# A two-layer decoder trunk on one core: the first projection by pairs of k-tiles, the heads in five steps, the input's second load later, six plain k-tiles at the borders

## The chip, the cores and the metric

The kernel runs on one core of a Trainium2 chip. The metric is the device time of one execution in microseconds (us), the median of several runs. The profile shown is that of one execution. Five engines work side by side, each through its own queue in order: TensorE (PE, matmuls, and PEld, its weight loads), VectorE (DVE), ScalarE (ACT), GpSimd (POOL) and SyncE (SP), which here issues every DMA.

## The reference, cut to what matters

Two layers, 256 tokens, width 2048, everything in float32. Layer 0 normalises the input, scales and shifts it by vectors made from a conditioning vector `c` (adaLN), multiplies it by one wide matrix and feeds two groups of four heads; layer 1 is a sparse attention. Each layer ends with an MLP.

```python
# adaLN vectors: silu(c) @ ada_w[l] + ada_b[l], six chunks of 2048 columns (shift, scale, gate, twice)
h = rms_norm(x, norm1_g) * (1 + scale) + shift
p = h @ w_in                                  # 256 x 2048 times 2048 x 8200
q_m, k_m (after conv+silu), v_m, o_m, if_m, q_r, k_r, v_r, g_r = split(p)
h_m = mlstm_chunkwise(q_m, k_m, v_m, gates(if_m))      # heads 0 to 3, width 256
h_r = retention_chunkwise(rotary(q_r), rotary(k_r), v_r)   # heads 4 to 7
y = rms_norm_per_head(concat(h_m, h_r)) * gate(o_m, g_r)
x = x + gate_vec * (y @ w_out)
x = x + gate_vec2 * (relu(mod(x) @ w1) ** 2 @ w2)     # then layer 1 likewise
```

## The kernel before

Weights come as k-tiles of 128 rows (16 of them, k = 0 to 15, for a width of 2048). A product in full precision is made in one of two ways. **Plain**: the float32 tile as it landed is multiplied at once (`mm`, line 124); the trace shows each such matmul as two instructions. **Split**: `wsplit` (lines 235 and 237) rounds the tile to `wh` on ScalarE and puts the rest into `wl` on VectorE, the activations `hs` are split likewise, and three fast matmuls (`wh` with both halves of `hs`, `wl` with the high one) give the result. Raw weights pass through four buffers `raw`, four `wh` and four `wl`; the plain tiles of the first stages use all three kinds in a fixed turn (`wraw`).

Stage by stage, with the names that the text uses:

- **Start.** x is loaded (`xn`), its row lengths are taken, it is scaled and transposed into `xT` (line 737). The adaLN shift and scale of the first norm come from 33.6 MB of `ada_w`, by pairs of k-tiles: for pair 0 to 7, `cond_sum` loads 4.2 MB in eight DMAs (`ar`, four buffers) and folds it on VectorE, 16 multiply-adds of 128x512 (lines 752 and 754); `cond_pair` then sums over partitions (four transposes on TensorE, four reductions on ScalarE, lines 335 and 338) and makes the two normalised k-tiles `hf` and their split `hs`.
- **Phase a**: plain products of k-tiles 0 to 3 with the columns of the values 0 to 2 and of one query (1792 columns), summed in PSUM over the four. **Phase b**: plain products of k-tiles 0 to 7 with the output gates and the last values (1536 columns). **Phase c**: all 16 k-tiles with the seven remaining q and k units (1792 columns), k-tiles 0 to 5 plain and 6 to 15 split. `gates()` (the small projection of the mLSTM gates, its scans and weights E) runs at k = 8. Pairs 2 to 7 are folded and normalised in between.
- **Rest of a**: k-tiles 4 to 15, split (12 steps). **Heads**: `segment` makes the remaining columns; when a head has q, k and gate, `mix_head` gives three steps (`scores`, `values`, `gated`), which are put into the list `pending`, and `side()` runs one of them after each piece of matmul work. `values` ends with a Newton square root on VectorE and the scaling `yn` on ScalarE (line 1005), `gated` with transposes of `yn` (line 1013). x is loaded again and transposed (lines 1151 to 1155) between two segments.
- **w_out**, the output projection, adds into `xT`. Meanwhile `Fill` spreads the folds of three more adaLN chunks (96 pieces of 512 KB, line 407) over its calls, one call per step of weights from k = 12 of phase c on.
- **Borders.** `entry` starts the three following projections (two MLPs and layer 1's input) before the norm's length is known: k-tiles 0 to 7 are multiplied plain and unnormalised (`wu`), the other eight split.

Of the kernel before, what the change touches and what calls it, by code (L numbers as in the profile page):

```python
# [23 lines left out]
EPS = 1e-6  # L24
NEG = -3.0e38
# [69 lines left out]
def tile_trunk(ctx: ExitStack, tc: tile.TileContext, io, out):  # L95
# [267 lines left out]
    def ada_rows(acc, hf):  # L363
# [17 lines left out]
        for c in (2 * hf, 2 * hf + 1):  # L381
            pending.extend(turn(c))
# [64 lines left out]
    class Norm:  # L447
# [53 lines left out]
    def entry(W, cols, tiles, norm, l, n, held, late, out, done):  # L501
# [5 lines left out]
        for k0 in range(0, 8, 2):  # L507
# [4 lines left out]
        for k0 in range(0, KT, 2):  # L512
            if k0 >= 8:
                wh, wl = wload(W, k0, 2, cols, PAIRED)
            for q, (c, m) in enumerate(tiles):
                for kk in range(2):
                    k = k0 + kk
                    if k < 8:
                        mm(held[q][0:m, 0:T + 1], ws[k0 // 2][:, kk * w + c:kk * w + c + m], us[k][:, 0:T + 1],
                           k == 0, k == 7)  # L520
                    else:
                        nmul2(q % 2)(late[q // 2], hs[k], wh, wl, kk * w + c, m, k == 8 and q % 2 == 0, k == KT - 1)
            side()
            if k0 == 6:
                for k in range(8, KT):
# [11 lines left out]
        for k in range(8):  # L537
            hs[k] = norm.normed(l, n, k)
        return hs

    def residual(W, nk, hget, gate, norm, groups, stag, fill):

        k0 = 0
        for plan, banks in groups:
# [77 lines left out]
    def mlp(l, before, fill, norm):  # L622
        with ExitStack() as es:
# [13 lines left out]
            def squared(i, a):  # L637
# [7 lines left out]
                       lambda q: squared(q, z[q]))  # L645
            for g in range(1, DFF // 512):
                def evac(j, b, g=g):
# [5 lines left out]
                       [[(j * P, P)] for j in range(4)], evac, banks1, fill=fill, first=8 if g == 1 else 0)  # L653
            if l == 1:
# [3 lines left out]
                zp.tile([P, 24], F32, name="pad")  # L658
# [32 lines left out]
    with ExitStack() as es:  # L691
# [24 lines left out]
        early = [load_ar(0, 0), load_ar(0, 1)]  # L716
# [6 lines left out]
        ss, v, r = st(4, "nv"), st(2, "nw"), st(2, "nr")  # L723
        for t in range(2):
# [31 lines left out]
        def cond_pair(pr):  # L756

            if pr not in sums_of:
                cond_sum(pr)
            acc = sums_of.pop(pr)  # L760
            cs = st(4, "adac")
            row_sums(cs, [acc[:, i // 2, (i % 2) * P:(i % 2 + 1) * P] for i in range(4)])
# [6 lines left out]
            out = {}  # L769
            for k in (2 * pr, 2 * pr + 1):  # L770
# [15 lines left out]

        for s in range(3):
# [3 lines left out]
        nb = sums(6)  # L791
        nb = [nb[2 * i:2 * i + 2] for i in range(3)]
        q0b = bank(2)
        hfs = {}
        for pr in range(PART // 2):
            ws = {}
            hfs.update(cond_pair(pr))
            for k in (2 * pr, 2 * pr + 1):
                ws[k] = [wraw() for _ in range(2)]
                for i, o, (a, b) in zip((0, 1, 1), (0, 0, 512), wcols):  # L800
                    SP.dma_start(ws[k][i][:, o:o + b - a], wE[k * P:(k + 1) * P, a:b])
            for k in (2 * pr, 2 * pr + 1):
# [11 lines left out]
        S.copy(q0, q0b)


        gbs = [lbank() for _ in range(4)]
        vbs = [bank(0), bank(1)]
        wc = {}

        def load_c(k):
            wc[k] = wplain(k, 3072, 4096), wplain(k, 6664, 7176)

        for k in range(PART):
            load_c(k)
            if k % 2 == 1:
                cond_sum((PART + k - 1) // 2)
        for k in range(HALF):
            if k not in wc:
                load_c(k)  # L830
            wa, wb = wc.pop(k)
            a, z = k == 0, k == HALF - 1
            for j in range(8):
                mm(gbs[j // 2][:, j % 2 * T:j % 2 * T + T], wa[:, j * P:(j + 1) * P], hfs[k], a and j % 2 == 0, z)
            for t in range(2):
                mm(vbs[t], hfs[k][:, t * P:(t + 1) * P], wb[:, 0:512], a, z)
            if k % 2 == 1 and k < PART:
                hfs.update(cond_pair((PART + k - 1) // 2))
            elif k % 2 == 1:
                cond_sum((PART + k - 1) // 2)  # L840
        gpart = []
        for j in range(4):
            gpart.append(xT[:, 2 * j:2 * j + 2, :])
            S.copy(gpart[j].rearrange("p e t -> p (e t)"), gbs[j])
        v3 = wp.tile([P, 2, 512], F32, tag="acc", bufs=2, name="v3")
# [550 lines left out]
```

## Time and profile before

| | before |
|---|---|
| median of 3 runs (lowest to highest) | 2325.82 us (2317.92 to 2327.18) |
| the profiled execution's own time | 2326.86 us |
| span from first to last instruction | 2325.1 us |
| TensorE busy share of the span | 97% |
| VectorE, ScalarE | 73%, 51% |
| data read | 607.38 MB |

The span lies inside the execution's own time; 1.8 us are around it. A busy share is an average over stages of different kinds, so stages are read by themselves. Matmuls are pipelined: the mean time of one is longer than the distance from one to the next.

### The profile page before, as it was taken

The numbers are of one execution on the slowest core, as the hardware profiler recorded it, in microseconds if no ns is written. First come the engines' busy times: TensorE is split into PE (matmuls) and PEld (weight loads), VectorE is DVE, ScalarE is ACT, GpSimd is POOL, SyncE is SP. The second block draws the span as 40 slices with busy tenths as digits, with TensorE's granted clock in tenths as the row PEclk, the third lists the DMA queues.
The fourth block names the chain that finished last, engine by engine and source line by source line (L and its number), as shares of the span: only waits on it lengthen the run. The fifth ranks groups of instructions, "written<-read, shape, count | busy, mean of one in ns | idle before, by whom it ended". The sixth has DMA issues, their size and how long they took to land.

```text
span 2325.1 us, 37502 instructions
## 1 busy us (share of the span) xinstructions
PE 2255.0 (97%) x14121; PEld 2008.9 (86%) x14121; DVE 1706.4 (73%) x2499; ACT 1190.4 (51%) x2248; POOL 0.5 (0%) x8
## 2 busy tenths in 40 slices
PE   5899998999999999999999999999999999999999
PEld 3688888999988888899989899999988888888887
DVE  5767897995878777888887789866877455555555
ACT  3225454455565565655555445665655555444443
POOL 0000000000000000000000000000000000000000
PEclk9999999999999999999999999999999999999999
DMA  9998998996699999999899787746878666555554
GB/s 330 353 305 284 304 319 270 329 328 218 215 318 314 317 312 317 307 310 315 279 328 318 251 268 228 247 137 188 272 263 292 182 194 195 190 190 199 191 190 162
DMA packets 268909, 611.97 MB, mean 263 GB/s; under 512 B 26692, under 2 KB 95286, under 8 KB 268728
## 3 DMA queue, kind: packets, MB, share of 16 engines
q1 hardware_dynamic: 268728, 609.59, 78.6%
q8 instruction: 110, 1.80, 0.3%
q14 instruction: 71, 0.58, 0.1%
HBM read 607.38 MB, written 2.12 MB: 262 GB/s over the span
## 4 chain that ended last, share of the span: by engine, by line
PE 81%; DVE 8%; DMA 7%; issue 2%; ACT 2%; SPq 0%; DVEq 0%; ACTq 0%
PE L L124 48%; PE M L124 31%; DMA ada<-in_ada_w_dram 3%; DVE wl L237 2%; DMA raw<-in_even_w_in_dram 2%; DVE acc L407 2%; DVE acc L754 1%; DMA raw<-in_mlp_w_dram 1%; PE M L335 1%; ACT wh L235 1%; DMA xn<-in_x_dram 0%; DVE cv L1065 0%; ACT junk L338 0%; PE M L737 0%; SPq L246 0%
## 5 line engine op out<-in xcount | busy, mean ns | idle before, releaser
L237 DVE TENSOR_TENSOR wl<-raw,wh 128x1024 fp32r<-128x1024 f32 (+1 forms) x724 | 877.6, 1214 | 485.1 <-ACT wh L235 474.9
L235 ACT CAST wh<-raw 128x1024 fp32r<-128x1024 f32 (+1 forms) x724 | 754.0, 1042 | 822.9 <-PE M L124 442.5
L124 PE MATMUL L<-hs,wh 128*128 128x256 f32 (+1 forms) x4608 | 1107.8, 321 | 6.7 <-ACT wh L235 4.4
L124 PE MATMUL L<-hs,wl 128*128 128x256 f32 x3120 | 866.3, 278 | 4.2 <-DVE wl L237 4.2
L124 PEld LDWEIGHTS L<-hs,wh 128*128 128x128 f32 x4608 | 762.2, 189 | 69.5 <-ACT wh L235 5.0
L124 PEld LDWEIGHTS L<-hs,wl 128*128 128x128 f32 x3120 | 587.9, 189 | 7.0 <-DVE wl L237 6.0
L124 PE MATMUL M<-hs,wh 128*128 128x512 f32 (+2 forms) x1816 | 514.8, 345 | 0.0
L124 PE MATMUL M<-hs,wl 128*128 128x256 f32 (+2 forms) x1444 | 401.4, 278 | 0.0
L407 DVE SCALAR_TENSOR_TENSOR acc<-ada,cond,acc 128x1024 f32<-128x1024 f32 x300 | 383.5, 1278 | 18.0 <-DMA ada<-in_ada_w_dram 17.7
L124 PEld LDWEIGHTS M<-hs,wh 128*128 128x128 f32 (+1 forms) x1816 | 313.0, 186 | 50.8 <-issue 1.6
L124 PEld LDWEIGHTS M<-hs,wl 128*128 128x128 f32 (+2 forms) x1444 | 268.9, 186 | 1.9 <-issue 1.1
L124 PE MATMUL L<-wh,zh 128*128 128x512 f32 x512 | 168.6, 389 | 0.0
L124 PE MATMUL M<-wh,zh 128*128 128x512 f32 x512 | 168.5, 389 | 0.0
L124 PEld LDWEIGHTS L<-wh,zh 128*128 128x128 f32 x512 | 96.1, 188 | 20.3 <-issue 0.4
L124 PEld LDWEIGHTS M<-wh,zh 128*128 128x128 f32 x512 | 96.1, 188 | 20.0
L124 PE MATMUL L<-wl,zh 128*128 128x512 f32 x256 | 99.7, 390 | 0.0
L124 PE MATMUL M<-wl,zh 128*128 128x512 f32 x256 | 99.6, 389 | 0.0
L338 ACT ACTIVATE junk<-M 128x128 f32<-128x128 f32 x210 | 55.1, 278 | 84.8 <-PE M L335 84.8
L754 DVE SCALAR_TENSOR_TENSOR acc<-ar,cond,acc 128x512 f32<-128x512 f32 x120 | 90.2, 751 | 5.0 <-DMA ar<-in_ada_w_dram 1.4
L638 ACT ACTIVATE half<-half 128x256 f32<-128x256 f32 x120 | 47.9, 411 | 24.2 <-DVE half L328 24.2
L124 PE MATMUL L<-hf,raw 128*128 128x256 f32 x224 | 53.3, 392 | 4.4 <-DMA raw<-in_even_w_in_dram 4.4
L124 PEld LDWEIGHTS L<-wl,zh 128*128 128x128 f32 x256 | 48.1, 188 | 10.2 <-DVE wl L237 0.3
(273 smaller groups left out, 1578.2 us busy)
## 6 DMA issues: line engine op xcount, KB each, us to landing
raw<-in_mlp_w_dram SPq DMA_DIRECT2D x504, 512.0 KB, 4.5
ada<-in_ada_w_dram SPq DMA_DIRECT2D x320, 512.0 KB, 5.3
raw<-in_even_w_in_dram SPq DMA_DIRECT2D x136, 256.0 KB, 5.2
ar<-in_ada_w_dram SPq DMA_DIRECT2D x64, 512.0 KB, 7.8
raw<-in_odd_w_in_dram SPq DMA_DIRECT2D x48, 512.0 KB, 4.5
raw<-in_even_w_out_dram SPq DMA_DIRECT2D x32, 512.0 KB, 5.2
raw<-in_odd_w_out_dram SPq DMA_DIRECT2D x32, 512.0 KB, 4.2
raw<-in_even_w_in_dram SPq DMA_DIRECT2D x28, 512.0 KB, 5.9
```

The lines of the kernel that those rows point to most:

```text
L124: PE.matmul(o, a, b, start=start, stop=stop, skip_group_check=True)
L235: S.copy(wh[:, :n], raw[:, :n])
L237: last_split[0] = V.tensor_tensor(wl[:, :n], raw[:, :n], wh[:, :n].bitcast(F32), op=OP.subtract)
L335: PE.transpose(b[:, i * P:(i + 1) * P], t, ident)
L338: S.activation(j, b[:, i * P:(i + 1) * P], func, accum_out=dst[:, i:i + 1])
L407: V.scalar_tensor_tensor(acc, r, cond[:, kr:kr + 1], acc, op0=OP.mult, op1=OP.add)
L638: S.activation(a, a, AF.Relu)
L754: V.scalar_tensor_tensor(acc, ar[:, kr], cc, acc, op0=OP.mult, op1=OP.add)
```

## The change

- **Start.** All eight `ar` DMAs of pair 0 are issued at once. Pair 0 is folded on TensorE: 16 plain matmuls whose stationary side is a column of `cond` repeated 32 times (`cond32`), the four of a group writing to four different 32-partition strips of one PSUM bank. The chain of a pair is cut in three: `folds` (loads and folds), `summed` (four matmuls with a column of ones in place of transposes and reductions), `normed`. They are called at separate places.
- **Phases a and b by pairs.** a for k-tiles 0, 1; b for 0, 1; a for 2, 3; b for 2 to 7. The sums of the first pair are copied out, those of the second added by VectorE (13 more additions of 128x512). Loads are called earlier (`load_a`, `load_b`).
- **Phase c.** k-tiles 0 to 3 plain, 4 to 15 split; loads called ahead by `load_q`; `folds` of pair 5, 6, 7 at k = 3, 6, 9, `summed` at k = 2, 5, 8, 11. `gates()` runs at k = 13 and ends after its scans; `score_weights` is called after phase c. `fill()` begins at k = 14, and `Fill` has 92 slots in place of 88.
- **Heads.** `values` no longer scales; a step `scaled` does, so a head has scores, values, scaled, gated (with the segment's product, five). x's second load and its transposes go into `pending` after the last segment and run within w_out, before its sums are added (`x_ready`). The segment of the last values comes after the first six retention units.
- **Borders.** `EARLY` = 6 plain k-tiles in `entry`, ten split. In the last MLP one transposition of the result's addend is called earlier (`turn(0)`).

```diff
+EARLY = 6
...
-            for k in range(8):
+            for k in range(EARLY):
...
-        early = [load_ar(0, 0), load_ar(0, 1)]
+        early = [load_ar(0, kq) for kq in range(4)]
...
+        def folds(pr):
+            acc = sums_of[pr] = sp0.tile([P, 2, T], F32, tag="acc0", bufs=3, name="acc0")
+            if pr == 0:
+                b = bank(3)
...
+                    if pr == 0:
+                        mm(b[32 * kr:32 * kr + 32, :], cond32(kq * 4 + kr),
+                           ar[:, kr].rearrange("p c t -> p (c t)"), kq == 0, kq == 3)
...
+        def summed(pr):
+            acc = sums_of.pop(pr)
+            cs = sums_of[-1] = bank(3)[:, 0:4]
+            for i in range(4):
+                mm(cs[:, i:i + 1], acc[:, i // 2, (i % 2) * P:(i % 2 + 1) * P], one1 if pr else quad, i == 0, i == 3)
...
+        folds(0)
+        summed(0)
+        normed(0)
+        load_a(0, 1)
+        folds(1)
+        load_b(0, 1)
+        load_a(2, 3)
+        values_queries(0)
+        gates_values(0, True, False)
+        summed(1)
+        normed(1)
+        gates_values(1, False, True)
...
+        folds(2)
+        load_b(2, 3)
+        values_queries(2)
+        gates_values(2, True, False)
+        summed(2)
+        normed(2)
+        load_b(4, 5)
+        folds(3)
+        gates_values(3, False, False)
+        load_b(6, 7)
+        gates_values(4, False, False)
+        gates_values(5, False, False)
+        summed(3)
+        normed(3)
...
+        load_q(0, 1)
+        gates_values(6, False, False)
+        load_q(2, 3)
+        folds(4)
+        gates_values(7, False, True)
...
-        fill = Fill([(0, 2), (0, 3), (0, 4)], 88, lag=False)
+        fill = Fill([(0, 2), (0, 3), (0, 4)], 92, lag=False)
...
-            if k >= 12:
+            if k >= 14:
                 fill()
                 fill()
-            if k == 8:
+            if k == 13:
                 SP.dma_start(c1, io["c1"])
-                gates()
+                gated_ = gates()
+            if (k, 0) not in wq:
+                load_q(k)
...
-                    if k < 6:
+                    if k < PART:
...
+            if k in (2, 5, 8, 11):
+                summed(4 + k // 3)
+            if k in (3, 6, 9, 12):
+                normed(3 + k // 3)
+                if k < 12:
+                    load_q(k + 1, k + 2)
+                    folds(4 + k // 3)
...
+    def scaled(x_):
+        yn, nb_, f = x_["yn"]
         for t in range(2):
             S.activation(yn[:, t, :], nb_[t][:, 0:T], AF.Copy, scale=f[:, t:t + 1])
...
-            pending.extend([None, a0, a1, None, b0, None, None, b1, None, None, None, g0, None, None, None, g1])
+            pending.extend([None, a0, a1, None, b0, None, None, None, s0, b1, None, g0, None, s1, None, g1])
...
+    pending.insert(6, lambda: x_half(0))
```

The order of instructions on three engines shows what the code only implies.

On TensorE, at the start, from the transposes of the second bank of x to the first matmul of phase a (`xn` x, `rows` parameter vectors, `acc` and `ar` the conditioning sums and their weights). Before:

```order
L737 MATMUL M_194<-c_78,xn 128x128 x4
L165 MATMUL M_129<-c_78,rows 128x128
L737 MATMUL M_174<-c_78,xn 128x128 x4
L737 MATMUL M_200<-c_78,xn 128x128 x4
L165 MATMUL M_132<-c_78,rows 128x98
L737 MATMUL M_180<-c_78,xn 128x128 x4
L737 MATMUL M_206<-c_78,xn 128x128 x4
L335 MATMUL M_250<-c_78,acc_226 128x128 x4
L124 MATMUL L<-raw,hf 128x512 x4
```

Now:

```order
L744 MATMUL M_202<-c_78,xn 128x128 x4
L125 MATMUL M_228<-ar,cond 32x512 x16
L166 MATMUL M_135<-c_78,rows 128x128
L125 MATMUL M_246<-quad,acc_227 128x1 x4
L744 MATMUL M_182<-c_78,xn 128x128 x4
L744 MATMUL M_208<-c_78,xn 128x128 x4
L166 MATMUL M_138<-c_78,rows 128x98
L744 MATMUL M_188<-c_78,xn 128x128 x4
L125 MATMUL L<-raw,hf 128x512
```

The 16 folds stand between the two halves of x's transposes, and the sum of pair 0 stands ahead of the second half.

On SP, the DMA issues of phase c's first half (`raw` the weights, 896 columns each, two per k-tile; `ar` the conditioning weights). Before:

```order
L711 DMA ar<-in_ada_w_dram 128x4x256 x8
L784 DMA raw<-in_even_w_in_dram 128x896 x12
L711 DMA ar<-in_ada_w_dram 128x4x256 x8
L246 DMA raw<-in_even_w_in_dram 128x896 x2
L711 DMA ar<-in_ada_w_dram 128x4x256
```

Now:

```order
L803 DMA raw<-in_even_w_in_dram 128x896 x8
L716 DMA ar<-in_ada_w_dram 128x4x256 x8
L247 DMA raw<-in_even_w_in_dram 128x896 x2
L716 DMA ar<-in_ada_w_dram 128x4x256 x2
L247 DMA raw<-in_even_w_in_dram 128x896 x2
L716 DMA ar<-in_ada_w_dram 128x4x256 x6
L247 DMA raw<-in_even_w_in_dram 128x896 x4
```

The eight plain tiles are those of k = 0 to 3; the pairs of line 247 are k = 4 and k = 5, and six of pair 5's eight conditioning loads stand behind the loads of k = 5.

On ScalarE, the first two mLSTM heads (`yn,hm` the squares, `yn<-M,hf` the scaling, `wh` the rounding of weights for TensorE). Before:

```order
L988 ACTIVATE yn,hm<-M_2858 128x256
L988 ACTIVATE yn,hm<-M_2859 128x256
L235 CAST wh<-raw 128x1024 x4
L1005 ACTIVATE yn<-M_2763,hf 128x256
L1005 ACTIVATE yn<-M_2764,hf 128x256
L1005 ACTIVATE yn<-M_2858,hf 128x256
L1005 ACTIVATE yn<-M_2859,hf 128x256
```

Now:

```order
L1058 ACTIVATE yn,hm<-M_2961 128x256
L1058 ACTIVATE yn,hm<-M_2962 128x256
L236 CAST wh<-raw 128x1024 x3
L1079 ACTIVATE yn<-M_2820,hf 128x256
L1079 ACTIVATE yn<-M_2821,hf 128x256
L236 CAST wh<-raw 128x1024 x2
L1115 ACT_TABLE_LOAD
L1115 ACTIVATE gate<-gate 128x512
L236 CAST wh<-raw 128x1024 x2
L1079 ACTIVATE yn<-M_2961,hf 128x256
L1079 ACTIVATE yn<-M_2962,hf 128x256
```

Four more weight roundings stand between the scaling of the first head and that of the second.

## Rows read from the trace of the kernel before

**Rows 1.** The page's first part: busy time, share of the span, instructions by engine.

```profile
PE 2255.0 (97%) x14121; PEld 2008.9 (86%) x14121; DVE 1706.4 (73%) x2499; ACT 1190.4 (51%) x2248; POOL 0.5 (0%) x8
```

**Rows 2.** Busy time by stage: stretch, length, engines, granted clock, DMA share, GB/s.

```profile
0.00:33.40 33.40, 10.57 (x39) 7.18 (x39) 17.45 (x40) 13.75 (x29) 0.38 (x7) 1.00 0.91 304
33.40:114.00 80.60, 71.35 (x241) 45.29 (x241) 58.16 (x89) 18.22 (x60) 0.00 (x0) 0.97 1.05 355
114.00:220.00 106.00, 101.55 (x654) 90.22 (x655) 76.67 (x124) 42.59 (x86) 0.00 (x0) 0.96 0.90 297
220.00:280.00 60.00, 59.45 (x300) 50.27 (x299) 47.21 (x57) 29.23 (x37) 0.00 (x0) 1.00 0.92 303
280.00:508.00 228.00, 208.69 (x1634) 200.21 (x1633) 207.02 (x357) 114.33 (x236) 0.11 (x1) 0.98 0.93 310
508.00:593.70 85.70, 85.66 (x745) 85.05 (x745) 54.06 (x80) 42.84 (x84) 0.00 (x0) 1.00 0.74 245
550.00:575.00 25.00, 25.00 (x220) 24.86 (x219) 14.64 (x18) 15.37 (x30) 0.00 (x0) 1.00 0.60 189
```

**Rows 3.** Timeline of all engines, 0 to 60: start, length, engine, line, work [idle before].

```profile
14.84 4.21 PE L737 MATMUL M<-c,xn 128*128 128x128 f32 x16 [7.47 <-DVE xn L733]
...
33.41 5.42 PE L124 MATMUL L<-raw,hf 128*128 128x512 f32 x8 [2.26 <-ACT hf L772]
...
35.36 11.78 DVE L754 SCALAR_TENSOR_TENSOR acc<-ar,cond,acc 128x512 f32<-128x512 f32 x15
...
50.11 5.40 PE L124 MATMUL L<-raw,hf 128*128 128x512 f32 x8 [2.26 <-ACT hf L772]
...
57.93 2.31 PE L124 MATMUL L<-raw,hf 128*128 128x512 f32 x5
```

**Rows 4.** Timeline of TensorE, 60 to 330, phases b and c.

```profile
63.94 3.62 PE L124 MATMUL L<-hf,raw 128*128 128x256 f32 x16
...
69.11 3.62 PE L124 MATMUL L<-hf,raw 128*128 128x256 f32 x16
...
89.50 0.66 PE L335 MATMUL M<-c,acc 128*128 128x128 f32 x4 [2.55 <-DVE acc L754]
...
113.99 6.08 PE L124 MATMUL L<-hf,raw 128*128 128x256 f32 x16 [4.43 <-DMA raw<-in_even_w_in_dram]
...
122.49 3.62 PE L124 MATMUL L<-hf,raw 128*128 128x256 f32 x16
...
128.53 3.62 PE L124 MATMUL L<-hf,raw 128*128 128x256 f32 x16
```

**Rows 5.** Timeline of TensorE, 1395 to 1400: plain matmuls in pairs of 64-row strips.

```profile
1396.15 0.92 PE L124 MATMUL M<-ik,iq 64*128 64x256 f32 x8
1397.01 0.50 PE L124 MATMUL L<-hs,wh 128*128 128x256 f32 x2
```

**Rows 6.** Waits, 280 to 510: who for whom, us in total, times, longest.

```profile
ACT yn L1005 <- DVE hf L180: 15.2, 3, 9.9
...
PE M L1013 <- ACT yn L1005: 8.2, 4, 3.3
...
PE L L124 <- ACT wh L235: 3.5, 1, 3.5
...
PE L L124 <- DVE hf L180: 2.3, 1, 2.3
```

**Rows 7.** VectorE's costliest group, 280 to 508: count, busy us, mean ns, idle before.

```profile
L407 DVE SCALAR_TENSOR_TENSOR acc<-ada,cond,acc 128x1024 f32<-128x1024 f32 x62 | 79.1, 1277 | 2.5 <-DMA ada<-in_ada_w_dram 2.3
```

**Rows 8.** One group of TensorE by form: the transposes of x's second load.

```profile
L1154 PE MATMUL M<-c,xn 128*128 128x128 f32 x32 | 4.9, 311 | 0.6 <-ACT xT L1155 0.6
```

**Rows 9.** Timeline of all engines at the first border, 588 to 616.

```profile
593.71 2.76 PE L124 MATMUL M<-hs,wu 128*128 128x257 f32 x12
...
601.88 1.31 ACT L496 ACTIVATE hs<-half,mod 128x256 fp32r<-128x256 f32 x3 [1.48 <-DVE half L494]
```

**Rows 10.** Timeline of TensorE there: the first split matmul of the border.

```profile
608.75 0.59 PE L124 MATMUL L<-hs,wh 128*128 128x256 f32 x2
```

More of the change, by code (lines that the diff above doesn't have):

```diff
@@ L506, in entry @@
         ws = []
-        for k0 in range(0, 8, 2):
+        for k0 in range(0, EARLY, 2):
             r = wp.tile([P, ROOM], F32, tag=("wh", "wl")[k0 // 2 % 2], bufs=4, name="wu")
@@ L723, in tile_trunk @@
         ss, v, r = st(4, "nv"), st(2, "nw"), st(2, "nr")
+        quad = small.tile([P, 1], F32, tag="quad", bufs=1, name="quad")
+        V.reduce_sum(quad, c0[:, 0:128:32], axis=AX.X)
         for t in range(2):
@@ L814, in tile_trunk @@
[L814 to L840, printed above, removed]
@@ L841, in tile_trunk, with gates_values @@
-        gpart = []
+                       k == k0 and e == 0, k == k0 + 1)
+            for s in range(3):
+                for t in range(2):
+                    (put_v(v_of[s], t, nb[s][t]) if k0 == 0 else add_v(s, t, nb[s][t]))
+            if k0 == 0:
+                S.copy(q0, q0b)
+            else:
+                V.tensor_tensor(q0, q0, q0b, op=OP.add)
+        gbs, vbs = [None] * 4, [None] * 2
+        def gates_values(k, first, last):
+            if first:
+                gbs[:] = [lbank() for _ in range(4)]
+                vbs[:] = [bank(0), bank(1)]
+            a_, b_ = wb.pop(k)
+            for j in range(8):
+                mm(gbs[j // 2][:, j % 2 * T:j % 2 * T + T], a_[:, j * P:(j + 1) * P], hfs[k], first and j % 2 == 0, last)
+            for t in range(2):
+                mm(vbs[t], hfs[k][:, t * P:(t + 1) * P], b_[:, 0:512], first, last)
@@ new lines, in flat @@
+        def flat(j):
+            return xT[:, 2 * j:2 * j + 2, :].rearrange("p e t -> p (e t)")
+        gpart = [xT[:, 2 * j:2 * j + 2, :] for j in range(4)]
+        folds(0)
[10 more added lines that the diff above has]
+        gates_values(1, False, True)
+        g23 = wp.tile([P, 2, 512], F32, tag="acc", bufs=2, name="g23")
@@ new lines, in tile_trunk, with load_q @@
+        load_b(2, 3)
[11 more added lines that the diff above has]
+        normed(3)
+        wq = {}
+        def load_q(*ks):
+            for k in ks:
+                for i in range(2):
+                    c = 256 + 896 * i
+                    wq[k, i] = wplain(k, c, c + 896) if k < PART else wload(wE, k, 1, [(c, c + 896)])
@@ L958, in mix_head @@
         x_ = {}
-        return (lambda: scores(x_, qt, kt, weight, ml), lambda: values(x_, v, ml), lambda: gated(x_, hd, gate))
+        return (lambda: scores(x_, qt, kt, weight, ml), lambda: values(x_, v, ml), lambda: scaled(x_),
+                lambda: gated(x_, hd, gate))
     def scores(x_, qt, kt, weight, ml):
@@ L1169, in yget, with x_loads, x_turn, x_half @@
         return ys[k]
+    turned_x = []
+    def x_loads(c):
+        out = []
+        for t in range(2):
+            tag, n = (("hraw", 2), ("cv", 2), ("qk", 5), ("qk", 5))[c]
+            p = mp.tile([P, 2, T], F32, tag=tag, bufs=n, name="xn").rearrange("p e t -> p (e t)")
+            SP.dma_start(p, x[t * P:(t + 1) * P, c * 512:(c + 1) * 512])
+            out.append(p)
+        return out
+    def x_turn(c, t, p):
+        b = bank()
+        for i in range(4):
+            PE.transpose(b[:, i * P:(i + 1) * P], p[:, i * P:(i + 1) * P], ident)
+        S.copy(xT[:, 4 * c:4 * c + 4, t * P:(t + 1) * P], b.rearrange("p (k t) -> p k t", k=4))
+        turned_x.append(c)
+    pieces = {}
+    def x_half(h):
+        for c in (2 * h, 2 * h + 1):
+            pieces[c] = x_loads(c)
+    pending.insert(6, lambda: x_half(0))
+    for h in range(2):
+        if h:
+            pending.extend([lambda: x_half(1), None, None, None])
+        for c in (2 * h, 2 * h + 1):
+            for t in range(2):
+                pending.extend([lambda c=c, t=t: x_turn(c, t, pieces[c][t]), None])
+    def x_ready(k):
+        while turned_x.count(k // 4) < 2:
+            side()
     nrm = Norm()
-    residual(io["even_w_out"][0], KT, yget, shift(0, 2), nrm, out_groups(), 2, fill)
+    residual(io["even_w_out"][0], KT, yget, shift(0, 2), nrm, out_groups(), 2, fill, x_ready)
     fill.flush()
```

126 lines of the change are left out of this document (59 added, 67 removed).

## The prediction

> **What bounds the kernel now.** The page first: TensorE is busy for 97% of the span, so only what shortens its work or its gaps counts [rows 1]. Next, busy time by stage. From 508 on TensorE is filled; a stretch of 25 us holds 220 matmuls of 256 columns, 0.114 us each [rows 2]. The gaps lie ahead of that: 22.8 us before the first matmul of phase a, 9.3 from there to phase c, 4.5 in phase c, 19.3 in the heads (length less TensorE's busy time in each stage). In the same stages DMA moves 297 to 355 GB/s and VectorE is busy for 207 of the heads' 228 us. So three engines are near their limits there, and time taken from one comes back only as far as the other two allow. I take 355 GB/s, the best stage, as what DMA can give.
>
> Then the timeline, for what the gaps wait for. Phase a starts at 33.41 behind the chain of pair 0, waits again at 50.11 for pair 1, and runs at half speed at each start: eight half matmuls take 5.4 us there [rows 3] where sixteen of half the width, the same columns, take 3.6 [rows 4]. The granted clock of that stage is 0.97 [rows 2]; the slow stretch follows a TensorE that stood or only transposed, so I read it as the 1.2 GHz level. Phase c starts after 4.43 us of waiting for weights [rows 4].
>
> **Prices.** A plain matmul of 256 columns costs 0.43 us: a k-tile of phase a is 14 such units, 57.93 to 63.94, 6.01 us [rows 3, 4]. A k-tile of phase b is 12 (5.17, from 63.94 to 69.11), of phase c plain 14 (6.04, from 122.49 to 128.53) [rows 4]. Split, 42 matmuls of 0.114: 4.8 us.
>
> **Start and phases a, b: about -15 us.** Pair 0's folds leave VectorE, where 15 take 11.8 us, for TensorE [rows 3]. The trace has no matmul on strips of 32 output columns. Its nearest row is the indexer: two plain matmuls of 256 and two of 128 columns, alternating between two strips of 64 rows, take 1396.15 to 1397.01, 0.86 us, where one after the other they would take 1.29 [rows 5]. That is just what comes out when the second half of each runs beside the first half of the next. By this the 16 folds of 512 columns (two halves of 0.43) take 17 x 0.43 = 7.3 us; one after the other 13.7; four abreast 3.4. I take 7.3, since the row is of the same kind of instruction, and add 2 us for the slow level. They begin at 19.05, when the first 16 transposes end [rows 3], end at 28.4, and with copy, sum, two small VectorE steps and the scaling phase a starts near 31.5.
>
> The Trainium skill ("TensorEngine Tiling (Array Packing)", Tiling Modes) has four independent 128x32 tiles, and its Key Properties say that changing the tiling mode drains the array. By the four tiles the folds take 3.4 us and phase a starts at 27.6; the row above shows only neighbours overlapping, and no run here shows a drain.
>
> What counts more is what follows. Before, a(2, 3) waited for pair 1. Now b(0, 1) stands ahead of it, so TensorE has 22 us of work while VectorE folds pair 1. From 31.5 on it has 4 x 6.01 + 8 x 5.17 = 65.4 us of work; I add 2 for pair 3, whose weights land about 82 at 355 GB/s, as its sums are wanted. Phase c then starts at 99, not 114. The 13 added VectorE sums (about 0.7 each) lie behind matmuls. Folds one after the other give -9, four abreast -17, as the weights of b(0, 1) land only about 44.
>
> **Phase c: about +1.5 us.** Two k-tiles fewer are plain: 2 x (6.04 - 4.8) = -2.5. Work falls from 89.9 to 87.4 us (6 for the gates in both), while 106 were used [rows 2]. But it starts 15 us earlier and DMA does not: three times, one pair's conditioning (4.19 MB) and three k-tiles (2.75 MB) must come in 14.3 us of matmuls, and at 355 GB/s they need 19.6. The queue makes it worse: the raw buffers of k = 5 are those of plain k = 3, so SP stands until about 123, with six of pair 5's loads behind. I take 5.3 us for each of the three, and 4 for restarts at the slow level: 20 us of waits where 16 were lost before. Phase c ends at 206.5 (220 before): together -13.5. If DMA keeps ahead the waits shrink to 4; if each triple waits twice as long they are 36. The gates, moved to k = 13, cost what they cost at k = 8.
>
> **Rest of a: 0.** 12 steps, 60 us at full TensorE [rows 2], as before.
>
> **Heads: about -12 us.** ScalarE stood 15.2 us behind the square roots, and TensorE 14.0 for it: 8.2 at the transposes of `yn`, 3.5 for rounded weights, 2.3 at the end [rows 6]. Four roundings now come between two scalings, so the 3.5 goes; the 8.2 only in part, since `gated` follows `values` after as many steps as before or fewer. The x loads (2.1 MB) leave, and three fills of 512 KB: calls 17 to 76 at 96/90 each make 64, where calls 21 to 80 at 96/86 made 67. DMA thus has 3.7 MB less, 12 us at the 310 GB/s of this stage; VectorE has 3 x 1.28 = 3.8 us less [rows 7]. I take DMA's 12: 216 us, which leaves VectorE 13 us of room. Ends: 0, if VectorE's chain stays as late as it is; -25, if VectorE alone bounds.
>
> **w_out: about +4.** The 32 transposes of x (4.9 us busy [rows 8]) come into a stage where TensorE has no gap [rows 2]. Eight fills more add 10 us to VectorE's 54 of 86: hidden. x itself must be there only before the sums are added, some 40 us later.
>
> **Borders: about -2.** Two k-tiles by four units go from 0.43 to 3 x 0.114: -0.7 each at three borders. The plain cover shrinks by 3.4 us: at the first border it ran from 593.7 to 608.75 and would end at 605.3, and the first normalised tiles are there by 603.2 [rows 9, 10]. With no such slack it would cost up to 2 us each. `turn(0)` moves 4 transposes within filled time: 0.
>
> **Sum.** -13.5 - 12 + 4 - 2.2 = -23.7, say -24. Against the profiled execution, 2325.1 of span and 1.8 around it, this gives 2303; that execution lies 1 us over the median, so 2302.
>
> **Rivals.**
> - *Folds one after the other* in the array: 6 us later at the start, a third of it lost in phase c's waits anyway: -18, 2308. For it: nothing here shows 32-column strips side by side. Chance 0.1.
> - *DMA keeps ahead in phase c.* Before, DMA moved only 297 GB/s there [rows 2], and loads are called two k-tiles ahead. Waits of 4 in place of 20: -40, 2286. Against it: SP's queue in order. Chance 0.2.
> - *It does not do what it says*: the start's gain is given back. DMA gives only 310, each triple waits 8 us, and the heads stay at 228 since VectorE, at 207, sets their pace: -15 + 9 + 4 - 2 = -4, 2322. For it: in the heads VectorE hardly waits for loads [rows 7]. Chance 0.17.
> - *Slower: PSUM banks of the heads.* Between `values` and `scaled` a head now holds one or two of the four M banks for three or four more steps, 4 to 5 us; whoever wants the bank waits on TensorE, and all matmuls behind it. It decides from 3 us a head (8 x 3 = 24). At 5 us: +16, 2342. Against it: the list is run in order and the four banks go round, so that two heads' steps mostly find a free one. Chance 0.08.
>
> **How the numbers follow.** The forecast has 0.45, the rivals 0.1, 0.2, 0.17 and 0.08. 0.5%, some 12 us, is about what a measurement of this kernel can tell from no change. Faster is forecast, first and second rival: 0.75; the third is within it: 0.17; the fourth 0.08. The likeliest case by itself runs from 2290 to 2313 (phase c's waits and the heads' ends by half). The range goes down to 2282, past the second rival, and up to 2323, past the third; the fourth is left out.
>
> **What would show it.** The first matmul of phase a at 31 to 32, with the folds taking 9 to 10 us before it; 38 says one after the other. The first of phase c near 99. In phase c, idle TensorE ahead of k = 6, 9 and 12 behind VectorE's folds or weights. The heads' stage near 216 us with fewer waits of TensorE for `yn`, its DMA near 310 GB/s. w_out some 4 us longer, each border 0.7 shorter. I am wrong if phase c waits for nothing, or if the heads take as long as before.

## The result and the profile after

| | before | after |
|---|---|---|
| median, us | 2324.24 (2317.92 to 2327.41, 13 runs) | 2315.22 (2308.74 to 2317.91, 13 runs) |
| ratio, 95% interval | | 0.9948, 0.9938 to 0.9958 |
| profiled execution, us | 2326.86 | 2312.93 |
| its span, granted clock | 2325.1, 0.994 | 2311.2, 0.994 |

The change makes the kernel 0.5% faster: 9.0 us by the two medians, about 12 by the ratio and 13.9 by the two spans. The forecast was 24 us, 2302; its range held the time.

The page's first part says little, as in [rows 1]: TensorE is busy for 97% of a shorter span.

```profile
PE 2252.9 (97%) x14237; PEld 2009.2 (87%) x14237; DVE 1709.1 (74%) x2504; ACT 1186.3 (51%) x2182; POOL 0.5 (0%) x8
```

Busy time by stage, the changed kernel's stretches that answer to [rows 2]: the start, phases a and b, phase c, the rest of a, the heads, w_out.

```profile
0.00:28.90 28.90, 12.61 (x72) 7.13 (x73) 7.26 (x27) 12.91 (x22) 0.38 (x7) 0.98 0.88 283
28.90:103.80 74.90, 71.66 (x254) 47.26 (x254) 45.54 (x72) 13.56 (x27) 0.00 (x0) 0.96 0.99 337
103.80:215.70 111.90, 99.47 (x693) 92.17 (x692) 88.69 (x132) 38.78 (x56) 0.00 (x0) 0.94 0.91 302
215.70:277.20 61.50, 61.50 (x298) 49.93 (x297) 52.65 (x75) 35.75 (x49) 0.00 (x0) 1.00 0.89 290
277.20:486.00 208.80, 197.05 (x1566) 189.64 (x1565) 197.09 (x339) 105.23 (x206) 0.11 (x1) 0.99 0.95 317
486.00:585.10 99.10, 96.93 (x824) 95.04 (x823) 70.38 (x104) 51.14 (x109) 0.00 (x0) 1.00 0.83 288
```

Phase c begins 10.2 us earlier (103.8, was 114.0) and ends only 4.3 earlier (215.7, was 220.0): it takes 111.9 us, was 106. Most of the gain lies in the heads, though less of it than the rows of the heads seem to show (228.0, now 208.8), since the border to w_out is cut at another place of the program there. Cut alike, from the last add of `v` to the last rotation, the heads took 220.6 us and now take 208.4, before and after:

```profile
282.10:502.70 220.60, 201.31 (x1583) 193.14 (x1582) 200.25 (x346) 110.34 (x229) 0.11 (x1) 0.98 0.94 313
```

```profile
279.30:487.70 208.40, 196.65 (x1563) 189.24 (x1562) 196.69 (x343) 105.27 (x207) 0.11 (x1) 0.99 0.94 314
```

TensorE's timeline of the start, beside [rows 3, 4]; the first row, with 32 instructions, is the folds on strips of 32 columns.

```profile
18.93 4.56 PE L125 MATMUL M<-ar,cond 128*32 128x512 f32 x32
...
28.86 1.92 PE L125 MATMUL L<-raw,hf 128*128 128x512 f32 x2
...
44.73 5.35 PE L125 MATMUL L<-hf,raw 128*128 128x256 f32 x16 [2.16 <-DMA raw<-in_even_w_in_dram]
...
93.33 3.72 PE L125 MATMUL L<-hf,raw 128*128 128x256 f32 x16 [1.08 <-ACT hf L794]
...
103.77 3.62 PE L125 MATMUL L<-hf,raw 128*128 128x256 f32 x16
```

TensorE's waits in phase c. There are three groups, and the timeline has them at 140, 161 and 184, ahead of k = 6, 9 and 12.

```profile
PE L L125 <- ACT wh L236: 9.8, 3, 4.9
PE M L125 <- DVE acc L773: 2.4, 3, 0.9
```

SyncE's issues in the same stretch (start, length of the group, count):

```profile
77.10 22.03 SPq L803 DMA_DIRECT2D raw<-in_even_w_in_dram  x12
99.22 9.28 SPq L716 DMA_DIRECT2D ar<-in_ada_w_dram  x8
108.59 2.11 SPq L247 DMA_DIRECT2D raw<-in_even_w_in_dram  x2
110.79 1.75 SPq L716 DMA_DIRECT2D ar<-in_ada_w_dram  x2
...
120.53 1.34 SPq L247 DMA_DIRECT2D raw<-in_even_w_in_dram  x2
121.92 7.39 SPq L716 DMA_DIRECT2D ar<-in_ada_w_dram  x6
```

From 112.5 to 120.5 the queue stands at the raw tile of k = 5, with six loads of pair 5 behind it, as forecast; it stands again at 132.7 to 142.4 (k = 8) and 155.5 to 163.9 (k = 11). And it stands inside the first row: of its twelve tiles the last are query weights, and one waits 9.5 us for a buffer that matmuls still read, with pair 4's loads behind it. SyncE's wait (total, times, longest):

```profile
SPq L803 <- PE L L125: 9.8, 2, 9.5
```

The table has the places that every experiment below is read by, all from profiled executions: phase a's and phase c's first matmul, the last copy of `qkr` (phase c is done), the last add of `v` (the rest of a is done), the last rotation (w_out begins), the first matmul of border 1, and the span's end.

| | ratio | a | c | `qkr` | `v` | w_out | border 1 | end |
|---|---|---|---|---|---|---|---|---|
| before | | 33.4 | 114.0 | 221.1 | 282.1 | 502.7 | 593.7 | 2325.1 |
| after | 0.9948 | 28.9 | 103.8 | 216.8 | 279.3 | 487.7 | 585.1 | 2311.2 |
| e9, after again | 0.9950 | 29.2 | 101.9 | 216.7 | 280.4 | 488.8 | 585.8 | 2313.9 |
| e1, phases only | 1.0007 | 28.5 | 103.1 | 216.3 | 279.2 | 503.7 | 596.2 | 2324.1 |
| e5, rest only | 0.9990 | 33.4 | 114.0 | 220.4 | 281.1 | 496.5 | 592.1 | 2320.1 |
| e12, e5 and pace | 0.9968 | 33.1 | 114.6 | 222.1 | 284.3 | 494.6 | 590.4 | 2315.9 |
| e6, four steps | 0.9979 | 28.5 | 107.2 | 222.4 | 284.6 | 496.0 | 596.1 | 2323.4 |
| e7, x between | 0.9987 | 29.0 | 102.6 | 218.1 | 281.5 | 503.1 | 595.5 | 2322.8 |
| e3, no loads | 0.9913 | 28.2 | 103.2 | 200.8 | 263.4 | 475.5 | 572.0 | 2299.3 |
| e4, GpSimd's queue | 0.9985 | 28.9 | 107.7 | 224.1 | 286.6 | 496.8 | 594.0 | 2320.5 |
| e8, order | 0.9985 | 29.1 | 101.9 | 215.9 | 278.9 | 488.7 | 587.1 | 2312.6 |
| e10, pair 4 early | 0.9937 | 29.4 | 102.6 | 214.4 | 276.6 | 486.9 | 583.7 | 2311.2 |
| e11, pair 4 too | 1.0020 | 28.2 | 113.1 | 230.8 | 294.0 | 503.9 | 601.5 | 2329.9 |

"Heads" below is `v` to w_out: 220.6 before, 208.4 after. Ratios are to the kernel before on the same chip. The executions of one kernel scatter by 2.5 to 17 us, so a profile's end and the median may differ: e6's profiled execution took 6.6 us more than its median, e7's 2.9 more, e8's 7.0 less. Eight of the kernels (after, e9, e1, e6, e7, e3, e4, e8) have the same code up to phase c, and it begins between 101.9 and 107.7.

### The profile page after: what moved, and what is told of

It reads as the page before. It is cut to its first block, busy times and chain, and to the rows that moved or that the text cites. A ratio compares the mean times of both kernels' runs of the same rounds, so it can differ in the third digit from the quotient of the medians.

```text
span 2311.2 us, 37700 instructions
## 1 busy us (share of the span) xinstructions
PE 2252.9 (97%) x14237; PEld 2009.2 (87%) x14237; DVE 1709.1 (74%) x2504; ACT 1186.3 (51%) x2182; POOL 0.5 (0%) x8
## 4 chain that ended last, share of the span: by engine, by line
PE 78%; DVE 9%; DMA 7%; ACT 2%; issue 2%; SPq 1%; DVEq 0%; ACTq 0%
PE L L125 47%; PE M L125 30%; DVE wl L238 3%; DMA raw<-in_even_w_in_dram 2%; DMA ar<-in_ada_w_dram 2%; DVE acc L773 1%; DVE acc L408 1%; DMA ada<-in_ada_w_dram 1%; ACT wh L236 1%; DMA raw<-in_mlp_w_dram 1%; SPq L716 1%; PE M L336 1%; DVE cv L1138 0%; DMA raw<-in_even_w_out_dram 0%; DVE half L495 0%
## 5 line engine op out<-in xcount | busy, mean ns | idle before, releaser
L238 DVE TENSOR_TENSOR wl<-raw,wh 128x1024 fp32r<-128x1024 f32 (+2 forms) x731 | 884.2, 1212 | 476.5 <-ACT wh L236 466.8
L236 ACT CAST wh<-raw 128x1024 fp32r<-128x1024 f32 (+2 forms) x731 | 760.6, 1042 | 870.9 <-PE M L125 442.1
L125 PE MATMUL L<-hs,wh 128*128 128x256 f32 (+1 forms) x4672 | 1119.5, 320 | 12.6 <-ACT wh L236 11.6
L125 PEld LDWEIGHTS L<-hs,wh 128*128 128x128 f32 x4672 | 770.6, 189 | 75.9 <-ACT wh L236 12.9
L125 PE MATMUL M<-hs,wh 128*128 128x256 f32 (+2 forms) x1856 | 520.6, 343 | 0.0
L125 PE MATMUL M<-hs,wl 128*128 128x256 f32 (+1 forms) x1464 | 406.4, 278 | 0.0
L125 PEld LDWEIGHTS M<-hs,wl 128*128 128x128 f32 (+1 forms) x1464 | 272.3, 186 | 1.5 <-issue 0.7
L773 DVE SCALAR_TENSOR_TENSOR acc<-ar,cond,acc 128x512 f32<-128x512 f32 x105 | 78.9, 751 | 7.5 <-DMA ar<-in_ada_w_dram 4.2
L339 ACT ACTIVATE junk<-M 128x128 f32<-128x128 f32 x178 | 46.8, 278 | 24.5 <-PE M L336 24.5
L125 PEld LDWEIGHTS L<-wl,zh 128*128 128x128 f32 x256 | 48.0, 188 | 10.2 <-DVE wl L238 0.3
L125 PEld LDWEIGHTS M<-wl,zh 128*128 128x128 f32 x256 | 48.1, 188 | 10.1
```

The costliest lines, as they stand in the source:

```text
L125: PE.matmul(o, a, b, start=start, stop=stop, skip_group_check=True)
L236: S.copy(wh[:, :n], raw[:, :n])
L238: last_split[0] = V.tensor_tensor(wl[:, :n], raw[:, :n], wh[:, :n].bitcast(F32), op=OP.subtract)
L339: S.activation(j, b[:, i * P:(i + 1) * P], func, accum_out=dst[:, i:i + 1])
```

## The experiments

Theory 1: each part works as forecast; the head start of 10 us is given back in phase c, as SyncE's queue stands at raw tiles with conditioning loads behind. Rivals: phase c is bound by its bytes alone, or by VectorE's folds; or the gain is not the phases' at all.

**The two halves.** In e1 heads, x and borders are undone; the new phases stay, with the pace of the fills and layer 1's turns:

```
-EARLY = 6
+EARLY = 8
...
-pending.extend([None, a0, a1, None, b0, None, None, None, s0, b1, None, g0, None, s1, None, g1])
+pending.extend([None, a0, a1, None, b0, None, None, b1, None, None, None, g0, None, None, None, g1])
...
-residual(io["even_w_out"][0], KT, yget, shift(0, 2), nrm, out_groups(), 2, fill, x_ready)
+residual(io["even_w_out"][0], KT, yget, shift(0, 2), nrm, out_groups(), 2, fill)
```

> Only the new first phases are kept: heads in four steps, x loaded and turned between two head segments, and eight plain k-tiles at the borders, all as before the change. Theory 1 (each part works by itself; the new first phases are worth the 3.3 us that they lead by where the heads begin, the rest comes from heads and borders): 3 us under the kernel before, 2321 us, ratio 0.9986. Rival 'the new start is worth nothing': 2324 us. Rival 'the heads are faster because the phases hand over earlier': 2312 us, nearly the whole gain.

Measured 2326.01 us, 1.0007 (0.9997 to 1.0018): nothing. The lead of 2.9 us at `v` is there and is lost in the heads, 224.5 us, where TensorE's wait for `yn` is 13.1 instead of the 8.2 of [rows 6]:

```profile
PE M L1082 <- ACT yn L1075: 13.1, 6, 3.6
```

The other half, e2: the kernel before, with heads, x, borders and turns of after, and after's 16 columns instead of 24 in `pad`, a tile ahead of the last stage's `zh` tiles.

```
+EARLY = 6
...
-zp.tile([P, 24], F32, name="pad")
+zp.tile([P, 16], F32, name="pad")
...
+lambda: scaled(x_),
...
+residual(io["even_w_out"][0], KT, yget, shift(0, 2), nrm, out_groups(), 2, fill, x_ready)
```

> The other half alone: the first phases of before, with the heads in five steps, x's later load, six plain k-tiles at the borders and the turns of layer 1 from after. Theory 1: heads -11.7, w_out +6.4, borders and what follows -5.3, together 10.6 us under the kernel before, 2314 us, ratio 0.9954. Rival 'the new start is worth nothing': the same as the whole change, 2312 to 2315 us. Rival 'the heads are faster because of the phases': 2323 us.

Measured 2334.52 us, 1.0044 (1.0032 to 1.0056). Up to border 3 it led by 6.4 us, then lost ten: the last 1,536 matmuls took 395 ns where e5, with the pad at 24 columns, has 389. One row of these matmuls (count, ns min/median/max, first and last start), of e2 and then of e5:

```profile
L125 PE MATMUL L<-wh,zh x512: 392/395/467, 1964.2 to 2321.2; 128*128 128x512 f32 x171
```

```profile
L125 PE MATMUL L<-wh,zh x512: 388/389/467, 1965.3 to 2312.4; 128*128 128x512 f32 x171
```

So e2 says nothing about the halves, and e5 takes its place:

```
-zp.tile([P, 16], F32, name="pad")
+zp.tile([P, 24], F32, name="pad")
```

> As e2_rest_only, with the pad tile in layer 1 at 24 columns, as in the kernel before, instead of 16. In e2_rest_only the last 512-column matmuls took 395 ns where both other kernels show 389, and the stage behind the third border was 10 us longer. Theory 'that tile's address makes it': 389 ns again, the stage behind the third border 714.6 us, the end 2318 to 2319 us, ratio 0.9972. Rival 'the new first phases make those 10 us': unchanged, 2334 us, ratio 1.004.

Measured 2322.25 us, 0.9990 (0.9979 to 1.0000); border 3 to the end 714.9 us (724.6 in e2, 714.6 before). The address theory holds: the pad is the only edit between the two. The changed kernel has 389 ns with 16 columns, so it isn't the pad's width as such. But now two halves worth nothing and 2 us stood against a whole worth 12.

**Is the whole really 12?** e9 is the changed kernel, unedited.

> The changed kernel itself, unedited, on the chip of the two runs below, since its parts by themselves (0.999 to 1.001 of the kernel before) don't add up to its own 0.9948. Theory 1 (the parts need each other): again 0.9938 to 0.9958. Rival 'part of the 0.9948 is this chip or these executions': 0.996 to 0.998.

Measured 2314.50 us, 0.9950 (0.9936 to 0.9963). It is; the parts need each other.

**Which part needs which.** e6 has four steps again, with all else of after: the scaling goes back to the end of `values`, and the lists of steps are the old ones.

```
-        x_["yn"] = yn, nb_, f
-    def scaled(x_):
-        yn, nb_, f = x_["yn"]
         for t in range(2):
             S.activation(yn[:, t, :], nb_[t][:, 0:T], AF.Copy, scale=f[:, t:t + 1])
...
```

> The changed kernel with the heads in four steps again (the scaling back at the end of values, the two old lists of steps); x's later load, the new phases and the borders stay. Theory 1 (the five steps take ScalarE's and TensorE's wait for yn away): TensorE's wait for yn 8 to 13 us instead of 2.4 in the heads, the end 6 to 10 us later than the changed kernel, 2321 to 2325 us. Rival 'the lighter load traffic in the heads makes the gain': within 3 us of 2315.

Measured 2318.59 us, 0.9979 (0.9969 to 0.9989): by the ratios 7 us over the changed kernel, as theory 1 had it, though by the medians, of two chips, 3.4. The heads' share in the profile is less, 211.4 us, with a wait for `yn` of 6.7, short of the 8 to 13 expected; w_out to border 1 has 100.1 instead of 97.4. e7 puts x's load, and the fourth pair of values, back where they were:

```
+v_of[3] = vtile()
+linear_n(wE, KT, 2, 6664, hget, lambda t, b: add_v(3, t, b, vpart), fill=fill, k1=HALF)
...
 segment(u("g", 4), u("q", 4))
+for t in range(2):
+    for q in range(2):
+        xn = wp.tile([P, 1024], F32, tag="raw", bufs=4, name="xn")
...
```

> The changed kernel with x loaded and turned between two head segments and the fourth pair of values ahead of the retention heads, both as before the change; five steps, phases and borders stay. Theory 1: heads 5 to 8 us longer (2.1 MB more at some 315 GB/s), w_out 6 us shorter, the end within 3 us of 2315. Rival 'the lighter load traffic in the heads makes the gain': heads 12 us longer, the end 6 us or more later, 2321 us or more.

Measured 2321.79 us, 0.9987 (0.9977 to 0.9998). Heads 221.6 us, w_out to border 1 92.4 instead of 97.4: 13 longer and 5 shorter, and by the ratios 9 us over the changed kernel, as the rival had it. TensorE's waits in the heads of e6, e7 and the changed kernel:

```profile
PE M L1082 <- ACT yn L1075: 6.7, 4, 2.5
```

```profile
PE M L1086 <- ACT yn L1079: 8.6, 5, 3.0
```

```profile
PE L L125 <- DVE wl L238: 6.5, 9, 1.4
PE M L1086 <- ACT yn L1079: 2.4, 3, 1.4
```

Five steps alone take 13.1 to 8.6 (e1 to e7), the later x alone 13.1 to 6.7 (e1 to e6), both 13.1 to 2.4. The wait for `yn` hangs on what the program puts between the steps, and x's move changes that as well as the bytes. e7 doesn't separate x's load from the values' move.

What e5 still lacks is the pace of the fills, an edit of one number each that the forecast had counted under DMA:

```
-fill = Fill([(0, 2), (0, 3), (0, 4)], 88, lag=False)
+fill = Fill([(0, 2), (0, 3), (0, 4)], 92, lag=False)
-            if k >= 12:
+            if k >= 14:
```

> As e5_rest_mend (first phases of before, all else of after), with the change's pace of the fills as well: calls from k = 14 instead of 12 in phase c, 92 slots instead of 88. The parts by themselves (e1 at 1.0007, e5 at 0.999) don't add up to 0.995, and e5's heads took 215.4 us where the whole change has 208.4, with 64 folds of ada instead of 63. Theory 'pace' (the fills crowd the heads of e5): heads 208 to 211 us, the end 4 to 7 us earlier than e5, ratio 0.996 to 0.9975. Rival 'the phases' hand-over' (what the new phases leave done or undone for the heads makes the 7 us): heads 214 us or more, ratio 0.9985 to 1.0.

Measured 2319.18 us, 0.9968 (0.9952 to 0.9984). Heads 210.3 us (e5 215.4): "pace" by both of its numbers, though the interval touches e5's. So heads, x, borders and pace make some 7 us with the old phases; the new ones add 4 to 5 (the intervals of e12 and of the changed kernel overlap a little), about the 2.8 to 4.3 by which they lead behind phase c. The wait for `yn` doesn't tell the heads' length by itself: e12 has 6.7 us of it, e5 5.6.

**What limits phase c.** e3 leaves 24 loads out:

```
+kept = []
...
-ar = early.pop(0) if early else load_ar(pr, kq)
+ar = early.pop(0) if early else load_ar(pr, kq) if pr < 5 else kept[kq]
+if pr == 4:
+    kept.append(ar)
```

> The changed kernel without the 24 conditioning loads of pairs 5 to 7 (12.6 MB); they are folded from pair 4's tiles instead, with every VectorE instruction kept. So k-tiles 10 to 15 get wrong conditioning. If transfers (by the queue's order or by their bytes) set phase c, it falls from 111.9 us to about 92 and PE's waits ahead of k = 6, 9 and 12 go; the end comes 15 to 20 us earlier, about 2296 us. If VectorE's folds set it (they stand ahead of the wl splits), phase c stays at 108 us or more and the end within 4 us of 2315.

Measured 2303.48 us, 0.9913 (0.9900 to 0.9925). Phase c in e3, cut at the last matmul, with all its folds: 96.5 us, a full clock, and 3.1 us of waits.

```profile
103.20:199.70 96.50, 93.31 (x694) 86.78 (x693) 87.53 (x132) 39.44 (x57) 0.00 (x0) 1.00 0.80 247
```

Its waits of TensorE:

```profile
PE M L125 <- DVE acc L776: 1.8, 2, 0.9
PE M L946 <- ACT gl L941: 1.3, 1, 1.3
```

VectorE's folds are ruled out as the bound: e3 has as many of them as the changed kernel. Transfers cost phase c 15 us; the end gains less, 8 us by the ratios and 12 by the spans. Whether it is their order or their bytes, e4, e8, e10 and e11 ask. e4:

```
-SP.dma_start(ar[:, :, c, :],
+(G if pr > 4 else SP).dma_start(ar[:, :, c, :],
...
```

> The conditioning loads of pairs 5 to 7 are issued by GpSimd's queue instead of SyncE's; bytes and folds are the same. Theory 1 (SyncE's queue stands at a raw tile that isn't free, with these loads behind it): issue gaps of some 26 us no longer hold them up, phase c falls from 111.9 to about 100 us, the end 8 to 12 us earlier, 2303 to 2307 us. Rival 'bytes' (the DMA engines carry no more than 300 GB/s in this stage): phase c 109 to 112 us, the end within 3 us of 2315. Rival 'VectorE's folds': the same as bytes.

Measured 2320.98 us, 0.9985 (0.9974 to 0.9995), 9 us worse than the changed kernel by the ratios. The conditioning loads no longer stand behind raw tiles and DMA is 7% faster, but the phase isn't:

```profile
107.70:223.00 115.30, 101.50 (x692) 93.79 (x691) 91.58 (x130) 39.21 (x56) 18.09 (x24) 0.93 0.95 324
```

TensorE's longest wait there:

```profile
PE M L125 <- DVE acc L773: 11.2, 4, 3.7
```

The waits for rounded weights (9.8 us) are gone as well; 11.2 us for the sums have come in their place. Weights, and the fills behind them, now take their share of the rate while the sums are what TensorE needs: SyncE issues the first fill at 116.0 (184.1 in the changed kernel), and up to the last copy of `qkr` 71.0 MB have moved, where the changed kernel has 67.6. e8 keeps SyncE and only changes the order:

```
-load_q(k + 1, k + 2)
+load_q(k + 1)
 folds(4 + k // 3)
+load_q(k + 2)
```

> The changed kernel with one call moved in phase c: at k = 3, 6 and 9 the weights of k + 1, then a pair's folds with its loads, then the weights of k + 2. So no conditioning load stands in SyncE's queue behind a raw tile that isn't free. Theory 1 (the queue's stops cost the phase): phase c 105 to 109 instead of 111.9 us, the end 3 to 6 us earlier, 2309 to 2312 us. Rival 'bytes' (weights for 12 k-tiles and three pairs' conditioning need the whole phase whatever their order): phase c 110 to 115 us, TensorE now waiting ahead of k = 5, 8 and 11 for weights, the end within 3 us of 2315.

Measured 2321.33 us, 0.9985 (0.9974 to 0.9996), 9 us worse than the changed kernel by the ratios, which neither side expected. The profiled execution, 2314.34, is among e8's fastest and doesn't show where they go: phase c from its first matmul to `qkr` takes 114.0 us there, where after and e9 have 113.0 and 114.8. No gain in any case, and no clean test: only pair 5's loads came free. SyncE now stands at the raw tiles of k = 7 (128.0 to 135.5) and k = 10 (148.3 to 157.8), each with seven loads of the next pair behind. Its issues from 128 to 142, where the view ends:

```profile
135.54 1.33 SPq L247 DMA_DIRECT2D raw<-in_even_w_in_dram  x2
136.92 6.33 SPq L716 DMA_DIRECT2D ar<-in_ada_w_dram  x6
```

e10 moves pair 4:

```
+folds(4)
 load_q(2, 3)
-folds(4)
```

> The changed kernel with one call moved: the folds of pair 4, with their eight loads, ahead of the query weights of k = 2 and 3. In the changed kernel SyncE stands at these weights from 89.6 to 99.2 us (their tiles are still read by matmuls), and DMA falls to 237 and 94 GB/s in 90 to 95 and 95 to 100. Theory 1 (the queue's stops cost phase c): pair 4's folds start near 97 instead of 106.6 us, the waits ahead of k = 6 to 12 shrink by some 6 us in all, phase c about 106 us, the end 4 to 7 us earlier than the changed kernel on this chip. Rival 'the raw tiles' (every later pair stands behind the next raw tile again, whatever pair 4 does): phase c 110 to 113 us, the end within 2 us.

Measured 2313.14 us, 0.9937 (0.9921 to 0.9954). The stop is closed. DMA from 90 to 95 and 95 to 100, of the changed kernel and then of e10:

```profile
90.00:95.00 5.00, 3.92 (x20) 2.92 (x19) 1.74 (x5) 1.69 (x4) 0.00 (x0) 1.00 0.60 237
95.00:100.00 5.00, 5.00 (x21) 3.66 (x20) 0.33 (x1) 0.00 (x0) 0.00 (x0) 1.00 0.36 94
```

```profile
90.00:95.00 5.00, 3.92 (x22) 3.40 (x21) 1.08 (x4) 1.69 (x4) 0.00 (x0) 1.00 1.08 362
95.00:100.00 5.00, 5.00 (x21) 3.65 (x20) 1.34 (x2) 0.00 (x0) 0.00 (x0) 1.00 1.10 348
```

That is 1.9 MB more in 10 us (5 x 125 and 5 x 254 GB/s), but phase c to `qkr` is 111.8 us, 1.2 to 3 shorter, and the median is 1.4 us under e9's on the same chip, with intervals that overlap: the rival "the raw tiles" had it so. It is the fastest version with the whole computation here, by a margin not secured. e11 puts pair 4 on GpSimd's queue as well (`pr > 3` in e4's line).

> As e4_c_pool, with pair 4's loads on GpSimd's queue as well, so that none of them stands behind weights. Theory 1: DMA above 340 GB/s from 90 to 175 us, and the phase 6 us shorter than in e4_c_pool (112.3), the end 3 to 6 us earlier than the changed kernel on this chip. Rival 'bytes': DMA above 340 GB/s too, but the weights now share the rate with the conditioning and TensorE waits for the sums instead; the end within 2 us of the changed kernel.

Measured 2331.04 us, 1.0020 (1.0010 to 1.0030): slower than before, and than either side expected. Pair 4's loads now compete with pair 3's and with phase b's weights. From 90 to 105 DMA runs at 357 to 373 GB/s and TensorE is busy for 8.5 of 15 us; phase c starts at 113.1. Theory 1, in the form "take away the stops and the time comes back", has fallen.

## Why the prediction was right, and its gain twice too large

- **Folds on TensorE.** Forecast 7.3 + 2 us, measured 4.56: too dear. Sixteen plain 512-column matmuls (32 instructions) one after the other would be 13.7 by the prediction's own price, four abreast 3.4. In the changed kernel the weight loads of the first groups of four start 0.86 us apart and those of later ones 0.43; the granted clock of the stretch is 1.00, so the slower start is read from the distances alone. In e9 the first 24 instructions take 2.78 us, where four abreast make 2.6, and the last eight wait for their loads:

```profile
18.41 2.78 PE L125 MATMUL M<-ar,cond 128*32 128x512 f32 x24
22.17 1.06 PE L125 MATMUL M<-ar,cond 128*32 128x512 f32 x8 [0.98 <-DMA ar<-in_ada_w_dram]
```

  The Trainium skill ("TensorEngine Tiling (Array Packing)", Tiling Modes) had the four independent strips; the trace agrees with it, not with the 64-row pairs of [rows 5]. Phase a starts at 28.9 (forecast 31.5).
- **Phases a and b.** Forecast 67.4 us, measured 74.9. In the rows: the wait of 2.16 for b(0, 1)'s weights, 1.7 lost as the 16 matmuls behind it took 5.35 instead of 3.62, three sets of sums at some 0.8, the wait of 1.08 for pair 3's `hf`, and x's last transposes in the first k-tile. The granted clock of those 16 matmuls, 44.7 to 50.0, is 0.68; e9, where they ran at full speed, needs 72.8 us. Phase c starts at 103.8 instead of 99.
- **Phase c.** The places were right: k = 6, 9 and 12, behind the raw tiles of k = 5, 8 and 11. It took 111.9 us, forecast 107.5: 87.4 of work and 20 lost in waits and slow restarts. The loss was sized well. e3 does the same matmuls at a full clock in 93.3 us of busy time, so 18.6 us of the 111.9 are lost: 12.4 of gaps, and 6 (an estimate, the rest) at the lower clock, whose mean was 0.94. The work was put too low, at 87.4 instead of 93.3: the four sums, some 0.8 us each, stand in no term; the other 2.6 are not split here.
- **The step that failed** is the sum of these, "together -13.5": it measured -4.3 (-2.8 at `v`). The start gave 2.6 us more than forecast, phases a and b took 7.5 more, phase c 4.4 more. What the sum had wrong is TensorE's own time and the way to phase c: seven sums of a pair, nearly 6 us, stand in no term, phase c's work was 2.6 us short besides, and the wait and the restart in b were not charged. It also read 106 less 89.9 as 16 us lost before, where [rows 2] have 4.5 us of gaps and a granted clock of 0.96; so it saw more to win in the old phase than there was.

  DMA fits this. To phase c's end the kernel moved 70.2 MB in 220 us before, 319 GB/s [rows 2], and 67.2 MB in 215.7 us after, 312 GB/s (rates by stage times lengths); without the fills issued by then, 13 and 7 of 0.52 MB, that is 63.4 and 63.5 MB. The new order moves no byte faster, and over the whole stretch neither comes near the forecast's 355 GB/s. That the bytes alone set the end isn't shown: e4 and e11 reached 317 and 324 GB/s up to phase c's end, and came there later. The rival "the start's gain is given back", at a chance of 0.17, named the outcome of this part; of its conditions DMA's rate came (302 GB/s), but TensorE waited 12.2 us for the three triples together, not 8 for each, and the heads didn't stay as long as they were.
- **Heads.** Forecast -12, measured -11.7 by the same borders (280.5 to 502.7 before, 277.2 to 487.7 after). DMA's rate stayed (313 and 315 GB/s) and the bytes fell by 3.2 MB, forecast 3.7. That the bytes alone did it is not shown, so the fit of the number may be luck: e6, e7 and e12 find the gain split over steps, x's place and the fills' pace, each with waits of its own. On TensorE, by the two rows of the heads above, it is 7.5 us of gaps (19.3 to 11.8) and 4.7 of work, about x's 32 transposes (4.9 us [rows 8]), which only moved to w_out. Open is why the old heads wait longer for `yn` behind the new phases (13.1, was 8.2), which is how e1 comes to nothing.
- **w_out.** Forecast +4, measured +6.4 (91.0 to 97.4): x's transposes are busy for 5.0 us, and 2.2 us of waits are new. e1 and e7, without x's turns there, have 92.5 and 92.4. Heads and w_out together give 5.3 us, forecast 8.
- **Borders.** Forecast -2.2. Border 1 to the end is 5.3 us shorter, but e1, which keeps eight plain k-tiles, has 3.5 of it, at 1727.9 us, and the kernels with six, e2 left out, lie between 1725.5 and 1728.4: the term is within the scatter. So of the 13.9 us by the spans 2.8 are gained up to `v`, 12.2 in the heads and 5.3 behind border 1, not all of it by the change, and w_out takes 6.4.
- **The rival of the PSUM banks** didn't come: it would have added 3 to 5 us a head, and TensorE's gaps in the heads fell by 7.5 us in all.

## What to carry to other kernels

Before moving work earlier, divide the bytes that the whole stretch must bring by the rate it has reached over all of it, stops included; here that sum didn't shrink, and most of the earlier start was given back. Price the small steps too: seven sums of 0.8 us, in no term here, are more than the lead of 4.3 us that was left. A stop in a queue also decides who gets the rate: in e4 and e11 taking it away starved the transfer that was needed next, so ask what the freed rate will carry. And test parts together as well as alone: two halves worth 0 and 2 us made 12.

## What the runs showed of the hardware beside that

A short wait can cost more than it lasts, and doesn't always. Nine profiles have the same wait of 1.08 us ahead of the same 16 matmuls, behind the same matmuls of phase b. In six of them, the changed kernel's among them, the 16 then took 3.72 us (93.33 above); in e1, e4 and e6 they took 5.41. e4's:

```profile
95.58 5.41 PE L125 MATMUL L<-hf,raw 128*128 128x256 f32 x16 [1.08 <-ACT hf L794]
```

The granted clock of e4 from 95 to 100 is 0.66, so most of this is time at 1.2 GHz, the lower of the two levels. The clock differs from one execution to the next: of e1's twelve, the three at a mean granted clock of 0.989 took 2330.2 us on average, the one at 0.995 took 2318.7. Part of the scatter within most kernels goes with it; e7's executions don't show it.

A tile's place in SBUF changed 512-column matmuls from 389 to 395 ns (e5 and e2, which differ by 8 columns of padding alone): 9 us over 1,536 of them.
